# Retention's sample queries: weighting and adding the states on ScalarE and VectorE, then summing by ones, in one core's decoder layer

## The chip, the cores and the metric

The kernel runs on one core of one Trainium2 chip. The metric is the device time of one execution in microseconds (us), the median of several runs. A profiled execution gives the trace from which all other times here are taken; its span runs from its first to its last instruction.

## The reference, cut to what matters

One layer of a hybrid decoder: a feed-forward block, a mixer (retention and HGRN2 side by side), an output projection and a second feed-forward block, for 272 prompt tokens and for 8 sample tokens, each of which has states of its own. The change is in the mixer's work for the 8 samples. For each of them, and for each of the 8 retention heads, a state S of 256 x 256 is updated, and the query reads the new state:

```python
o = jnp.einsum('bhij,bhjv->bhiv', inner, v) + jnp.einsum('bhid,bhdv->bhiv', q_dec, S)
S_new = jnp.exp(lg * C)[:, None, None].astype(S.dtype) * S + jnp.einsum('bhjd,bhjv->bhdv', k_dec, v)
```

With one token per sample (C = 1) the output is q times the new state: a sum over the 256 rows of the state, which lie as two chunks of 128 partitions. The new states are outputs too (`state_ret_sample`). All data is fp32.

## The kernel before, in words

Every large product is a stream of weight blocks. A unit of 8 blocks (128 x 1024, 512 KB) is loaded by SyncE's DMA queue (SP) into `raw`, ScalarE casts its high part into `whi` (L188), VectorE makes the low part `wlo` (L189), and TensorE makes three matmuls per block in L218: `whi` with the high and the low part of the activations, and `wlo` with the high part. `raw`, `whi` and `wlo` have three buffers each. Of a block TensorE reads `whi` first and `wlo` with the third matmul; the next `raw` load of a buffer waits until `wlo` was made from it.

In the mixer, `project` runs over the heads u = 0 to 7: six groups of the input projection (f, q_h, i_h, q_r, k_r, v_r), then four groups of gates of the head before (g_r with a_r, g_h with a_h, twice). A group has 16 steps (k), a step six matmuls, a unit of weights four steps. Beside it run threads, Python generators that `pump` calls once per step: `mix_hg(u)` starts behind i_h, `mix_ret(u)` behind v_r. `yield n` lets n steps pass. So TensorE's order is written out by these numbers; ScalarE's, VectorE's, GpSimd's and SP's orders are made by a scheduler that takes each instruction when it holds it for ready, whatever the step at which it was written.

`mix_ret` keeps the 8 states of a head as four tiles `smr` of 4 samples: `sms[2 * e + c]` has chunk c of samples 4e to 4e + 3. For each half e, ScalarE scales both tiles by the decay (L1192), VectorE adds value times key, sample by sample (L1198), and SP sends both to the output (L1202, `out_srs`). Later come the queries into the bank `pqr`: 16 matmuls (L1211) of 128 x 32 weights from `qdr`, one of whose 32 columns is the query's chunk, with 256 columns of state; four samples go to four 32-row quarters of the bank. `qdr` is zero but for these columns, which `alone` (L734) writes once per head. Behind the queries come the centring, the transposed outputs `por` and the norms; at the end `done_r` releases the gate's evacuation of the group g_r, and `done_h` that of g_h. `mix_hg` has the like for HGRN2: queries `pq` (L1039), then `po`, norms and `done_h`.

Of the kernel before, what the change touches and what calls it, by code (L numbers as in the profile page):

```python
# [13 lines left out]
AF = mybir.ActivationFunctionType  # L14
ALU = mybir.AluOpType
# [3 lines left out]
P = 128  # L19
# [4 lines left out]
NMETA, SEQ, NS = 16, 256, 8  # L24
# [27 lines left out]
ALONE = 4 * 32 + 1  # L52
# [76 lines left out]
def trunk(ctx: ExitStack, tc: tile.TileContext, A, O):  # L129
    nc = tc.nc  # L130
# [12 lines left out]
    def mx_bank(name):  # L143
        return ps_m.tile([P, 512], F32, tag="mx", name=name)
# [94 lines left out]
    def mul(out, a, b):  # L239
        nc.vector.tensor_tensor(out=out, in0=a, in1=b, op=ALU.mult)  # L240
# [306 lines left out]
    with tc.tile_pool(name="yp", bufs=1) as yp:  # L547
# [7 lines left out]
        with tc.tile_pool(name="mp", bufs=1) as mp:  # L555
# [7 lines left out]
            def tmp(name, shape=(P, T), bufs=1, dt=F32, tag=None):  # L563
                if name in rows:
                    rows[name] = rows[name][1:] + rows[name][:1]
                    return rp.tile(list(shape), dt, tag=rows[name][-1], name=name)
                return mp.tile(list(shape), dt, tag=tag or name, name=name, bufs=bufs)
# [19 lines left out]


            qdh = tmp("qdh", (P, 4, ALONE))
            qdr = tmp("qdr", (P, 4, ALONE))  # L590
            nc.gpsimd.memset(qdh, 0.0)
            nc.gpsimd.memset(qdr, 0.0)
            qdh_at = [qdh.rearrange("p a c -> p (a c)")[:, 256 * h :] for h in range(2)]
            qdr_at = [qdr.rearrange("p a c -> p (a c)")[:, 2 * ALONE * c :] for c in range(2)]
            vsm = tmp("vsm", (P, P))
            vt2 = tmp("vt2", (P, 2, P))
            scr2 = tmp("scr2", (P, NMETA))
# [50 lines left out]
            def evacuate(n, c0, c1, o0, o1, b0, b1):  # L648
# [14 lines left out]
                elif n == "i_h":  # L663
                    v = st.pop("i_h", None)
                    if v is None:
                        v = tmp("v", (P, 2, T))
                        nc.scalar.copy(v[:, 0, :], o0)
                        nc.scalar.copy(v[:, 1, :], o1)

                    start(mix_hg(c0 // 2, st["f"], st["k"], st["q"], v), {0: 20, 2: 46}.get(c0, 4))  # L670
                elif n in ("q_r", "k_r"):
                    sc, w, x0 = (1.0, TL, NMETA) if n == "q_r" else (KSC, T, 0)
# [9 lines left out]
                elif n == "v_r":  # L682
                    v = tmp("v", (P, 2, T))
                    nc.scalar.copy(v[:, 0, :], o0)
                    nc.scalar.copy(v[:, 1, :], o1)
                    start(mix_ret(c0 // 2, st["q_r"], st["k_r"], v), 24 if c0 == 2 else 3)
                elif n in ("g_r", "g_h"):
                    sg = tmp("gs", (P, TL), bufs=2)
                    t = tmp("gt", (P, TL), bufs=2)
                    nc.scalar.activation(sg, o0, AF.Sigmoid)  # L690
                    mul(t, sg, o0)
                    sa = tmp("gs", (P, TL), bufs=2)
                    nc.scalar.activation(sa, o1, AF.Sigmoid)
                    mul(t, t, sa)
                    u, e = divmod(c0, 2)
                    while u not in (done_r if n == "g_r" else done_h):
                        pump()
                    if n == "g_r":
                        y = tmp("y", (P, TL))
                        mul(y, t, on_r[u][:, e, :])  # L700
                        st["y"] = y
                    else:
                        y = st["y"]
                        nc.vector.scalar_tensor_tensor(
                            out=t, in0=t, scalar=ngt[:, c0 : c0 + 1], in1=on_h[u][:, e, :], op0=ALU.mult, op1=ALU.mult)

                        ys[c0] = y if c0 < EARLY else yp.tile([P, TL], F32, tag=f"y{c0}", name=f"y{c0}")
                        add(ys[c0], y, t)
                        if c0 < EARLY:
                            split(yh[c0], yl[c0], y)  # L710
# [22 lines left out]
            def alone(qd, q):  # L733
                nc.vector.tensor_copy(  # L734
                    qd[:, :, : 128 : 32].rearrange("p (c e) j -> p c e j", e=2),
                    q[:, :, SEQ:].rearrange("p c (e j) -> p c e j", e=2))
# [9 lines left out]
            def mix_hg(u, f, k, q, v):  # L746

                calm = 2
# [14 lines left out]
                sms, vbs = [], []  # L763
# [230 lines left out]
                def samples(h):  # L994
                    vb, sm = vbs[h], sms[h]
                    for b in range(NS):
                        at = NMETA + b
                        nc.scalar.activation(sm[:, b, :], sm[:, b, :], AF.Copy, scale=meta[:, h, at : at + 1])
                        nc.vector.scalar_tensor_tensor(
                            out=sm[:, b, :], in0=vb[:, b, :], scalar=meta[:, h, at + NS : at + NS + 1], in1=sm[:, b, :],  # L1000
                            op0=ALU.mult, op1=ALU.add)
                    nc.sync.dma_start(O["sgs"][2 * u + h], sm)
# [15 lines left out]
                for h in range(2):  # L1018
# [7 lines left out]
                    for b in range(2):  # L1026
                        nc.vector.scalar_tensor_tensor(
                            out=S[:, b + 1, :], in0=S[:, b, :], scalar=Tt[:, h, b : b + 1],
                            in1=pst[:, (b + 1) * P : (b + 2) * P], op0=ALU.mult, op1=ALU.add)
                    nc.sync.dma_start(O["sgp"][2 * u + h], S[:, 2, :])  # L1030
                if u == 1:
                    yield 2
                    samples(1)
                yield (8, 11, 45)[min(u, 2)]
                pq = mx_bank("pq")
                for h in range(2):
                    for b in range(NS):
                        j = 32 * (b % 4)
                        nc.tensor.matmul(  # L1039
                            pq[j : j + 32, :P], qdh_at[h][:, 32 * b : 32 * b + 32], sms[h][:, b, :],  # L1040
                            start=h == 0 and b < 4, stop=h == 1 and b >= 4, tile_position=(0, j))
# [26 lines left out]
                calm = calm if u else 0  # L1068
# [16 lines left out]
            def mix_ret(u, q, k, v):  # L1085
# [3 lines left out]
                calm = 2  # L1089
                sms = []  # L1090
# [13 lines left out]
                for c in range(2):  # L1104
# [22 lines left out]
                    for x, g, his, i, lo in todo:  # L1127
                        for hi in his:
                            nc.scalar.activation(hi, x, AF.Copy, scale=g)
                        nc.vector.scalar_tensor_tensor(  # L1130
                            out=lo, in0=x, scalar=g, in1=his[i].bitcast(F32), op0=ALU.mult, op1=ALU.subtract)
                    yield 2
                alone(qdr, q)
                vts = [vt[:, 0], vt[:, 1], vs2]
                vrow = rows_out(vt2.rearrange("p c f -> p (c f)")[16:24, :], 256, "vr")

# [25 lines left out]
                for c in range(2):  # L1162
# [9 lines left out]
                    if c == 0:  # L1172
                        gams = [tmp("gam", (P, 1))]
                        nc.gpsimd.tensor_scalar(
                            out=gams[0], in0=so[:, 0:1], scalar1=GAMMA[u], scalar2=GAMMA[u], op0=ALU.min, op1=ALU.max)
# [13 lines left out]
                for e in range(2):  # L1189
# [3 lines left out]
                    for i in (2 * e, 2 * e + 1):  # L1193
                        for c in range(2):
                            for b in (2 * i, 2 * i + 1):
# [3 lines left out]
                                    out=x, in0=vbs[i][:, b - 2 * i, :], scalar=kk, in1=x, op0=ALU.mult, op1=ALU.add)  # L1199
# [1 line left out]
                    for c in range(2):  # L1201
                        nc.sync.dma_start(O["srs"][u, c, :, 4 * e : 4 * e + 4, :], ss[c])  # L1202
                    yield 1 if e else 10 if u == 0 else 6
                yield (11 if u == 0 else 15) + 2 * calm
                pq = mx_bank("pqr")
                scores(pq[:, 256:], 2)
                for e in range(2):
                    for c in range(2):
                        for j in range(4):
                            b = 4 * e + j  # L1210
                            nc.tensor.matmul(  # L1211
                                pq[32 * j : 32 * j + 32, :256], qdr_at[c][:, 32 * b : 32 * b + 32],
                                sms[2 * e + c][:, j, :], start=e + c == 0, stop=e + c == 2, tile_position=(0, 32 * j))
                mul(scr2[:NB2], pq[:NB2, 256 : 256 + NMETA], dt[:NB2, c2:])
                upper_upper_lower(sc2, scr2[:NB2])
                os = tmp("osr", (P, 256))
# [160 lines left out]
```

## Time and profile before

| | |
|---|---|
| median of 3 runs | 2567.05 us (2566.23 to 2567.45) |
| span of the profiled execution | 2563.9 us |
| TensorE busy (modelled ends) | 2553.4 us, 23424 matmul records |
| VectorE busy | 1702.8 us, 66% |
| ScalarE busy | 1392.2 us, 54% |
| retention's queries, `pqr` (L1211) | 256 records, the first at 859.8, the last at 1698.6 us |
| out_srs (L1202) | 32 DMAs of 512 KB, 6.7 us to landing (median) |

The profiled execution's own time is its span; the runs' median stands 3.15 us above it. An fp32 matmul leaves two records. A matmul's record begins when the one before it is still in the array, so the pace is read from the starts: 0.113 us from one 264-column matmul to the next. A row of a timeline gives start, length, engine, line, operation, tiles and count; in brackets, how long the engine was idle before it and what ended that. Heads follow each other in 126 us; head 3's queries are at 1190.65 us.

### The profile page before, as it was taken

How to read it: one execution, taken by the hardware profiler on the slowest of the kernel's cores; microseconds unless marked ns; L12 is line 12 of the kernel's file. 1: busy time of each engine (PE TensorE's matmuls, PEld its weight loads, DVE VectorE, ACT ScalarE, POOL GpSimd, SP SyncE). 2: the span in 40 equal slices, each digit the busy share in tenths (PEclk: the TensorE clock that was granted, in tenths of full speed). 3: DMA queues.
4: the chain of work that ended last, by engine and by line, in shares of the span. 5: the costliest groups of instructions: out<-in, count | busy, mean ns of one | idle time of the engine just before them, and what ended most of it. 6: DMA issues, size and time to landing. Idle time of an engine off the chain costs nothing.

```text
span 2563.9 us, 56275 instructions
## 1 busy us (share of the span) xinstructions
PE 2553.4 (100%) x23424; PEld 2534.4 (99%) x23424; DVE 1702.8 (66%) x2827; ACT 1392.2 (54%) x2186; POOL 57.0 (2%) x152
## 2 busy tenths in 40 slices
PE   9999999999999999999999999999999999999999
PEld 9999999999999999999999999999999999999998
DVE  6444544475569878777777777777885555556555
ACT  5444444444456767767676666675564444444443
POOL 0000000000000000000000000000000000000000
PEclk9999999999999999999999999999999999999999
DMA  7555555555555876767676767675556565565554
GB/s 244 183 187 183 187 182 184 186 182 186 184 201 180 287 265 232 264 214 260 212 264 215 259 223 255 224 239 188 196 190 197 194 197 195 194 196 195 195 195 149
DMA packets 156897, 536.26 MB, mean 209 GB/s; under 512 B 17952, under 2 KB 25952, under 8 KB 156640
## 3 DMA queue, kind: packets, MB, share of 16 engines
q1 hardware_dynamic: 156352, 532.37, 62.0%
q8 instruction: 183, 3.00, 0.5%
q14 instruction: 74, 0.61, 0.1%
q10 hardware_dynamic: 288, 0.29, 0.0%
HBM read 501.99 MB, written 30.61 MB: 208 GB/s over the span
## 4 chain that ended last, share of the span: by engine, by line
PE 96%; DVE 2%; ACT 0%; issue 0%; DMA 0%; SPq 0%; ACTq 0%; DVEq 0%
PE up L218 36%; PE dn L218 19%; PE pj_i_h L218 3%; PE pj_g_r L218 3%; PE pj_q_h L218 3%; PE pj_g_h L218 3%; PE pj_a_r L218 3%; PE pj_a_h L218 3%; PE pj_f L218 3%; PE pj_q_r L218 3%; PE pj_k_r L218 3%; PE wo L218 3%; PE pj_v_r L218 3%; DVE wlo L189 1%; PE pqr L1211 1%; PE psr L1168 0%
## 5 line engine op out<-in xcount | busy, mean ns | idle before, releaser
L189 DVE TENSOR_TENSOR wlo<-raw,whi 128x1024 fp32r<-128x1024 f32 (+1 forms) x869 | 1062.2, 1223 | 740.7 <-ACT whi L188 737.3
L188 ACT CAST whi<-raw 128x1024 fp32r<-128x1024 f32 (+1 forms) x870 | 905.7, 1042 | 909.2 <-PE up L218 411.0
L218 PE MATMUL up<-xh,whi 128*128 128x280 f32 (+1 forms) x2624 | 725.6, 280 | 0.6 <-ACT whi L188 0.6
L218 PE MATMUL up<-xh,wlo 128*128 128x280 f32 (+1 forms) x2624 | 725.8, 280 | 0.4 <-DVE wlo L189 0.3
L218 PE MATMUL up<-xl,whi 128*128 128x280 f32 (+1 forms) x2624 | 725.4, 279 | 0.0
L218 PEld LDWEIGHTS up<-xh,wlo 128*128 128x128 f32 x2624 | 492.6, 189 | 1.0 <-DVE wlo L189 1.0
L218 PEld LDWEIGHTS up<-xh,whi 128*128 128x128 f32 x2624 | 492.6, 189 | 0.8 <-ACT whi L188 0.8
L218 PEld LDWEIGHTS up<-xl,whi 128*128 128x128 f32 x2624 | 492.6, 189 | 0.0
L218 PE MATMUL dn<-hh,whi 128*128 128x280 f32 (+1 forms) x1376 | 384.7, 280 | 0.0
L218 PE MATMUL dn<-hh,wlo 128*128 128x280 f32 (+1 forms) x1376 | 384.3, 279 | 0.0
L218 PE MATMUL dn<-hl,whi 128*128 128x280 f32 (+1 forms) x1376 | 384.3, 279 | 0.0
L218 PEld LDWEIGHTS dn<-hh,whi 128*128 128x128 f32 x1376 | 260.1, 189 | 0.1
L218 PEld LDWEIGHTS dn<-hl,whi 128*128 128x128 f32 x1376 | 260.1, 189 | 0.1
L218 PEld LDWEIGHTS dn<-hh,wlo 128*128 128x128 f32 x1376 | 260.1, 189 | 0.0
L218 PE MATMUL pj_k_r<-xh,whi 128*128 128x280 f32 x256 | 74.2, 290 | 0.0
L218 PE MATMUL pj_g_r<-xh,whi 128*128 128x264 f32 x256 | 74.0, 289 | 0.0
L218 PE MATMUL pj_v_r<-xh,whi 128*128 128x280 f32 x256 | 73.8, 288 | 0.0
L218 PE MATMUL pj_v_r<-xh,wlo 128*128 128x280 f32 x256 | 72.4, 283 | 0.3 <-DVE wlo L189 0.3
L218 PE MATMUL pj_g_h<-xh,whi 128*128 128x264 f32 x256 | 72.7, 284 | 0.0
L218 PE MATMUL pj_k_r<-xh,wlo 128*128 128x280 f32 x256 | 72.4, 283 | 0.0
L218 PE MATMUL pj_v_r<-xl,whi 128*128 128x280 f32 x256 | 72.3, 283 | 0.0
L218 PE MATMUL pj_k_r<-xl,whi 128*128 128x280 f32 x256 | 72.3, 283 | 0.0
(421 smaller groups left out, 5263.4 us busy)
## 6 DMA issues: line engine op xcount, KB each, us to landing
raw<-in_w_up SPq DMA_DIRECT2D x343, 512.0 KB, 4.1
raw<-in_w_in SPq DMA_DIRECT2D x320, 512.0 KB, 4.3
raw<-in_w_dn SPq DMA_DIRECT2D x172, 512.0 KB, 3.5
smr<-in_sr SPq DMA_DIRECT2D x32, 512.0 KB, 5.0
out_srs<-smr SPq DMA_DIRECT2D x32, 512.0 KB, 6.7
raw<-in_w_out SPq DMA_DIRECT2D x32, 512.0 KB, 3.9
vbr<-vrd SPq DMA_DIRECT2D x32, 256.0 KB, 4.1
smh<-in_sg SPq DMA_DIRECT2D x16, 512.0 KB, 5.2
```

Of the source, the lines that this page charges most:

```text
L188: nc.scalar.copy(hi[:, j:jn, :], raw[:, j:jn, :])
L189: nc.vector.tensor_tensor(out=lo[:, j0:j1, :], in0=raw[:, j0:j1, :], in1=hi[:, j0:j1, :].bitcast(F32), op=ALU.subtract)
L218: nc.tensor.matmul(o, w, t, start=start, stop=stop)
L1211: nc.tensor.matmul(pq[32 * j : 32 * j + 32, :256], qdr_at[c][:, 32 * b : 32 * b + 32], sms[2 * e + c][:, j, :], start=e + c == 0, stop=e + ...
```

## The change

For each half e, ScalarE multiplies chunk 0 of each sample's state by the query of that chunk (a scalar per partition), in place, and VectorE multiplies chunk 1 by its query and adds. TensorE then only sums over the partitions: one matmul per sample, with a table `one` whose 32 columns are zero but for the column of half e. The queries stand 32 steps behind the states' update instead of 15 (head 0) or 19; HGRN2's queries stand 13 steps later in heads 2 to 7, so that both still stand at the same step there.

```diff
             qdh = tmp("qdh", (P, 4, ALONE))
-            qdr = tmp("qdr", (P, 4, ALONE))
+            one = tmp("one", (P, 2, 32))
             nc.gpsimd.memset(qdh, 0.0)
-            nc.gpsimd.memset(qdr, 0.0)
+            nc.gpsimd.memset(one, 0.0)
+            for e in range(2):
+                nc.gpsimd.memset(one[:, e, e : e + 1], 1.0)
...
-                yield (8, 11, 45)[min(u, 2)]
+                yield (8, 11, 58)[min(u, 2)]
                 pq = mx_bank("pq")
...
-                alone(qdr, q)
...
-                yield (11 if u == 0 else 15) + 2 * calm
+                yield 18 + 2 * calm
+                for e in range(2):
+                    s0, s1 = sms[2 * e : 2 * e + 2]
+                    for b in range(4):
+                        g = [q[:, c, SEQ + 4 * e + b : SEQ + 4 * e + b + 1] for c in range(2)]
+                        nc.scalar.activation(s0[:, b, :], s0[:, b, :], AF.Copy, scale=g[0])
+                        nc.vector.scalar_tensor_tensor(
+                            out=s0[:, b, :], in0=s1[:, b, :], scalar=g[1], in1=s0[:, b, :], op0=ALU.mult, op1=ALU.add)
+                    yield 5
                 pq = mx_bank("pqr")
                 scores(pq[:, 256:], 2)
                 for e in range(2):
-                    for c in range(2):
-                        for j in range(4):
-                            b = 4 * e + j
-                            nc.tensor.matmul(
-                                pq[32 * j : 32 * j + 32, :256], qdr_at[c][:, 32 * b : 32 * b + 32],
-                                sms[2 * e + c][:, j, :], start=e + c == 0, stop=e + c == 2, tile_position=(0, 32 * j))
+                    for j in range(4):
+                        nc.tensor.matmul(
+                            pq[32 * j : 32 * j + 32, :256], one[:, e, :], sms[2 * e][:, j, :],
+                            start=e == 0, stop=e == 1, tile_position=(0, 32 * j))
```

The order of instructions around head 3's queries, by engine. Lines behind L600 have other numbers in the changed kernel: the weighting is L1209, the sum L1210, the query matmul L1217. First TensorE before, in the group g_r of gates (`pj_g_r` and `pj_a_r` are its banks, `xh` and `xl` the activations by step):

```order
L218 MATMUL pj_a_r_15214<-xh_10_9275,whi_15276 128x264
L218 MATMUL pj_a_r_15214<-xl_10_9276,whi_15276 128x264
L218 MATMUL pj_a_r_15214<-xh_10_9275,wlo_15277 128x264
L1039 MATMUL pq<-smh,qdh 32x128 x16
L1141 MATMUL pqr<-q_r,k_r 16x16 x2
L1211 MATMUL pqr<-smr,qdr 32x256 x16
L218 MATMUL pj_g_r_15213<-xh_11_9279,whi_15276 128x264
```

And TensorE in the changed kernel, in the group g_h behind it:

```order
L218 MATMUL pj_a_h_15375<-xh_7_9265,whi_15415 128x264
L218 MATMUL pj_a_h_15375<-xl_7_9266,whi_15415 128x264
L218 MATMUL pj_a_h_15375<-xh_7_9265,wlo_15416 128x264
L1040 MATMUL pq<-smh,qdh 32x128 x16
L1141 MATMUL pqr<-q_r,k_r 16x16 x2
L1217 MATMUL pqr<-smr,one 32x256 x8
L218 MATMUL pj_g_h_15374<-xh_8_9269,whi_15485 128x264
```

The queries have moved from behind step 10 of g_r to behind step 7 of g_h, and 8 of 16 matmuls are left. Next ScalarE before, from the casts of two units of weights to the queries' evacuation (`osh`; `gs` is a gate's sigmoid):

```order
L188 CAST whi_15216<-raw_15215 128x8x128
L188 CAST whi_15246<-raw_15245 128x8x128
L690 ACTIVATE gs<-pj_g_h_15035 128x264
L188 CAST whi_15276<-raw_15275 128x8x128
L693 ACTIVATE gs<-pj_a_h_15036 128x264
L188 CAST whi_15354<-raw_15353 128x8x128
L188 CAST whi_15395<-raw_15394 128x8x128
L1043 COPY osh<-pq 128x128
```

ScalarE in the changed kernel at the same place (`whi_15268` is the cast that was `whi_15246`):

```order
L188 CAST whi_15238<-raw_15237 128x8x128
L188 CAST whi_15268<-raw_15267 128x8x128
L1209 ACTIVATE smr<-smr,q_r 128x256
L691 ACTIVATE gs<-pj_g_h_15057 128x264
L188 CAST whi_15298<-raw_15297 128x8x128
L694 ACTIVATE gs<-pj_a_h_15058 128x264
L1209 ACTIVATE smr<-smr,q_r 128x256 x3
L188 CAST whi_15328<-raw_15327 128x8x128
L1209 ACTIVATE smr<-smr,q_r 128x256
L188 CAST whi_15377<-raw_15376 128x8x128
L1209 ACTIVATE smr<-smr,q_r 128x256 x3
L188 CAST whi_15415<-raw_15414 128x8x128
```

Each half's first weighting stands alone between two casts. VectorE in the changed kernel at this place (before, the same rows without L1210):

```order
L189 TENSOR_TENSOR wlo_15269<-raw_15267,whi_15268 128x8x128
L1198 SCALAR_TENSOR_TENSOR smr<-vbr,sro,smr 128x256 x3
L240 TENSOR_TENSOR gt<-gs,pj_g_h_15057 128x264
L1210 SCALAR_TENSOR_TENSOR smr<-smr,q_r 128x256
L189 TENSOR_TENSOR wlo_15299<-raw_15297,whi_15298 128x8x128
L240 TENSOR_TENSOR gt<-gt,gs 128x264
L1210 SCALAR_TENSOR_TENSOR smr<-smr,q_r 128x256
L705 SCALAR_TENSOR_TENSOR gt<-gt,ngt,on_h 128x264
L1210 SCALAR_TENSOR_TENSOR smr<-smr,q_r 128x256
L189 TENSOR_TENSOR wlo_15329<-raw_15327,whi_15328 128x8x128
```

The sums stand singly between the low parts. Last SP's queue before:

```order
L185 DMA raw_15275<-in_w_in 128x1024
L1202 DMA out_srs<-smr 128x1024
L185 DMA raw_15353<-in_w_in 128x1024
L1202 DMA out_srs<-smr 128x1024
L185 DMA raw_15394<-in_w_in 128x1024
L185 DMA raw_15463<-in_w_in 128x1024
L1202 DMA out_srs<-smr 128x1024
L185 DMA raw_15493<-in_w_in 128x1024
```

SP's queue in the changed kernel:

```order
L185 DMA raw_15297<-in_w_in 128x1024
L1202 DMA out_srs<-smr 128x1024
L185 DMA raw_15327<-in_w_in 128x1024
L1202 DMA out_srs<-smr 128x1024
L185 DMA raw_15376<-in_w_in 128x1024
L1202 DMA out_srs<-smr 128x1024
L185 DMA raw_15414<-in_w_in 128x1024
L185 DMA raw_15484<-in_w_in 128x1024
```

The third output, of the second half's first chunk, stands one weight load earlier.

More of the change, by code (lines that the diff above doesn't have):

```diff
@@ L589, in trunk @@
             qdh = tmp("qdh", (P, 4, ALONE))
-            qdr = tmp("qdr", (P, 4, ALONE))
+            one = tmp("one", (P, 2, 32))
             nc.gpsimd.memset(qdh, 0.0)
-            nc.gpsimd.memset(qdr, 0.0)
+            nc.gpsimd.memset(one, 0.0)
+            for e in range(2):
+                nc.gpsimd.memset(one[:, e, e : e + 1], 1.0)
             qdh_at = [qdh.rearrange("p a c -> p (a c)")[:, 256 * h :] for h in range(2)]
-            qdr_at = [qdr.rearrange("p a c -> p (a c)")[:, 2 * ALONE * c :] for c in range(2)]
             vsm = tmp("vsm", (P, P))
```

## The prediction

> **What bounds the kernel now.** I read the page first, then TensorE's waits, then the timelines of five engines around one head's sample queries.
>
> ```profile
> span 2563.9 us, 56275 instructions
> PE 2553.4 (100%) x23424; PEld 2534.4 (99%) x23424; DVE 1702.8 (66%) x2827; ACT 1392.2 (54%) x2186; POOL 57.0 (2%) x152
> PE 96%; DVE 2%; ACT 0%; issue 0%; DMA 0%; SPq 0%; ACTq 0%; DVEq 0%
> PE pt L1116 <- POOL tails L1103: 0.9, 1, 0.9
> PE pj_f L218 <- DVE wlo L189: 0.7, 1, 0.7
> PE pj_v_r L218 <- DVE wlo L189: 0.3, 1, 0.3
> PE psc L1141 <- DVE acch L836: 0.2, 1, 0.2
> ```
>
> The chain is TensorE for 96% of the span. The four wait rows are all of TensorE's waits between 740 and 1740 us (engine, what waited, releaser: total, times, longest), where all eight heads lie: 2.1 us. So TensorE work that goes comes off the end in full, and each new wait of TensorE is added in full. What can make it wait is the weight pipeline: raw block by DMA, its high part by ScalarE (whi, L188), its low part by VectorE (wlo, L189), three buffers of each. How near that is to failing is seen in head 3, around its queries:
>
> ```profile
> 1180.41 1.98 ACT L188 CAST whi<-raw 128x1024 fp32r<-128x1024 f32 x2
> 1182.99 0.39 ACT L690 ACTIVATE gs<-pj_g_h 128x264 f32<-128x264 f32 x1 [0.60 <-PE pj_g_h L218]
> 1185.35 1.05 ACT L188 CAST whi<-raw 128x1024 fp32r<-128x1024 f32 x1 [1.97 <-DMA raw<-in_w_in]
> 1184.59 1.22 DVE L189 TENSOR_TENSOR wlo<-raw,whi 128x1024 fp32r<-128x1024 f32 x1
> 1187.26 1.22 DVE L189 TENSOR_TENSOR wlo<-raw,whi 128x1024 fp32r<-128x1024 f32 x1
> 1185.83 0.28 PE L218 MATMUL pj_g_r<-xh,whi 128*128 128x264 f32 x1
> 1188.53 0.28 PE L218 MATMUL pj_g_r<-xh,whi 128*128 128x264 f32 x1
> 1188.75 0.28 PE L218 MATMUL pj_g_r<-xh,wlo 128*128 128x264 f32 x1
> 1190.65 1.08 PE L1039 MATMUL pq<-smh,qdh 128*32 128x128 f32 x32
> 1191.60 0.42 PE L1211 MATMUL pqr<-smr,qdr 128*32 128x256 f32 x3
> 1191.65 1.89 PE L1211 MATMUL pqr<-smr,qdr 128*32 128x256 f32 x29
> 1193.47 0.38 PE L218 MATMUL pj_g_r<-xh,whi 128*128 128x264 f32 x1
> ```
>
> Start, length, engine, operation. A block takes TensorE 1188.53 - 1185.83 = 2.70 us. The low part of the block of 1188.53 is done at 1188.48 and read at 1188.75: 0.27 us of lead. ScalarE is not busy there; it waits for the weights' DMA. Then the queries take TensorE from 1190.65 to 1193.47 without using weights, and the lead grows by 2.8 us. They stand where the pipeline is emptiest.
>
> **Part 1: fewer query matmuls.** They cost 1193.47 - 1191.60 = 1.87 us for 16 of 256 columns (32 records). Eight remain, of the same shape: 0.93 us less per head, 8 x 0.93 = 7.4 us off TensorE. Bounds: zero to 0.93 per head; I take the top, since the 29 records in 1.89 us are evenly paced. The Trainium skill, TensorEngine Tiling (Array Packing), Key Properties, says that changing the tiling mode drains TensorE. By this rule what is paid per change of mode isn't halved. The row of 1191.60 follows HGRN2's queries without a gap, so entering costs nothing there; leaving may be in the 0.38 of the last row, 0.1 more than the 0.28 of its neighbours. By the rule the sum would be (1.87 - 0.1) / 2 = 0.88 per head, 7.1 in all, instead of 7.4.
>
> The memsets of the table of ones come once, 64 elements wide instead of 516: nothing, on GpSimd, idle 98%. The copy into qdr goes:
>
> ```profile
> L734 DVE COPY qdr<-q_r 128x16 f32<-128x16 f32 x8 | 1.4, 176 | 0.0
> L998 ACT ACTIVATE smh<-smh,meta 128x128 f32<-128x128 f32 x128 | 41.1, 391 | 0.4
> L1192 ACT ACTIVATE smr<-smr,gam 128x1024 f32<-128x1024 f32 x16 | 17.6, 1142 | 9.2 <-POOL gam L1174 9.2
> L1198 DVE SCALAR_TENSOR_TENSOR smr<-vbr,sro,smr 128x256 f32<-128x256 f32 x64 | 27.5, 478 | 1.9 <-DMA vbr<-vrd 1.8
> ```
>
> **Part 2: eight weightings and eight sums per head.** The sum (L1210) has the form of L1198: 0.48 us, 0.40 when they follow each other (five took 2.06), so 3.2 to 3.8 us of VectorE per head. A weighting (L1209) of 256 lies between the rows of 128 and 1024 columns: 391 + 128 x (1142 - 391) / 896 = 498 ns, some 0.4 back to back: 3.2 to 4.0 us of ScalarE. Over a head of 126 us (the first out_srs of heads 3 and 4, below, lie 1306.54 - 1180.31 apart) there is room on both (66% and 54% busy). What counts is what these instructions wait for, and who stands behind them.
>
> **Part 3: the new wait.** A weighting overwrites the updated state, which must first have left by the output DMA (L1202). In the order of ScalarE, the first weighting stands between the cast of the block of 1185.83 and that of 1188.53, whatever the later yield says. The queue of the DMAs, and L1202's landings:
>
> ```profile
> 1179.92 0.33 SPq L185 DMA_DIRECT2D raw<-in_w_in  x1
> 1180.31 0.42 SPq L1202 DMA_DIRECT2D out_srs<-smr  x1
> 1182.72 0.33 SPq L185 DMA_DIRECT2D raw<-in_w_in  x1
> 1183.11 0.50 SPq L1202 DMA_DIRECT2D out_srs<-smr  x1
> 1185.84 3.00 SPq L185 DMA_DIRECT2D raw<-in_w_in  x2
> 1188.89 0.43 SPq L1202 DMA_DIRECT2D out_srs<-smr  x1
> 1306.54 0.42 SPq L1202 DMA_DIRECT2D out_srs<-smr  x1
> DMA to landing us min/median/max: 6.4/6.7/7.3
> ```
>
> First wait, by ScalarE's and VectorE's new order. The state's first chunk is issued at 1180.31, as before, and lands at 6.4 (the least, since it is the first of four): 1186.7. Weighting 0.4, gs 0.3 (0.39 less the overlap with its neighbours), cast 1.05, low part 1.25 with the hand-over: 1189.7. VectorE's gt and first sum run beside the cast. TensorE wants it at 1188.75: it waits 0.95 us.
>
> Second wait. In SP's new order the second half's first chunk goes ahead of the second of the two raw loads of 1185.84; it is issued at about 1186.25 instead of 1188.89 and lands at the median 6.7: 1192.95. The weighting of the second half stands ahead of the cast for the block after next: 0.45 + 1.05 + 1.25 = 2.75, done at 1195.7. TensorE, no longer held up by queries, would read it at 1188.75 + 2 x 2.70 = 1194.15, with the first wait 1195.1: it waits 0.6 more. The casts of the raw blocks behind it have their DMAs landed by then. Then the queries come (13 steps of 0.68 us later) and the lead is back.
>
> So a steady head pays 1.55 and saves 0.93. Heads 2 to 7 have this order; I take head 3 for all six. Head 0 has its own:
>
> ```profile
> 854.47 0.80 SPq L1202 DMA_DIRECT2D out_srs<-smr  x1
> 857.19 1.05 ACT L188 CAST whi<-raw 128x1024 fp32r<-128x1024 f32 x1
> 859.89 1.05 ACT L188 CAST whi<-raw 128x1024 fp32r<-128x1024 f32 x1 [0.83 <-DMA raw<-in_w_in]
> 865.45 0.28 PE L218 MATMUL pj_q_r<-xh,wlo 128*128 128x264 f32 x1
> ```
>
> There four weightings stand between the casts of 857.19 and 859.89 and wait for 854.47 + 6.7 = 861.2; four of 0.4, a copy and K's copy (0.9), cast and low part (2.3) end at 866.0. TensorE would read them at 865.45 less the 1.9 us of queries that have moved away: 863.55. It waits 2.5 us. Head 1 I take as a steady one, 1.55, between nothing and head 0's.
>
> **Part 4: HGRN2's queries later.** From 45 to 58 steps in heads 2 to 7: the same 16 matmuls, still right ahead of retention's. Bound: nothing where the lead holds, up to 2.8 us per head where the cover is gone; that loss is already in the first two waits. Nothing waits for the results sooner: mix_ret of head 7 ends 75 steps after its start where 80 are had, mix_hg 131 of 144. What moves with them (centring, norms, output transposes) costs the same; the row below shows the next thin place.
>
> ```profile
> 1219.81 1.22 DVE L189 TENSOR_TENSOR wlo<-raw,whi 128x1024 fp32r<-128x1024 f32 x1
> 1218.33 1.22 DVE L189 TENSOR_TENSOR wlo<-raw,whi 128x1024 fp32r<-128x1024 f32 x1
> 1220.86 0.28 PE L218 MATMUL pj_f<-xh,wlo 128*128 128x280 f32 x1
> ```
>
> The low part ends at 1219.55 and is read at 1220.86: 1.3 us of lead under the norms' work, which now falls some 9 us later. I take no wait there, with up to 1.5 us per head as the bound.
>
> **Sum.** Heads 2 to 7: 6 x (1.55 - 0.93) = 3.7; head 0: 2.5 - 0.93 = 1.6; head 1: 0.6. Together 5.9 us more: the span goes from 2563.9 to 2569.8. The median of the runs before, 2567.05, lies 3.15 above the span; with that, 2573.0.
>
> **Rivals.** (a) *The output lands in time.* If the first chunk lands within 5.4 us instead of 6.4, the second half's within 5.1 and head 0's within 4.2, no wait is left: 2567.05 - 7.4 = 2559.6. For it, other DMAs of 512 KB do:
>
> ```profile
> raw<-in_w_in SPq DMA_DIRECT2D x320, 512.0 KB, 4.3
> raw<-in_w_dn SPq DMA_DIRECT2D x172, 512.0 KB, 3.5
> ```
>
> Against it: L1202's least is 6.4. The Trainium skill, DMA: Bandwidth & Descriptors, Anatomy of one DMA, fits 2.0 us plus bytes over 436 GB/s (for the GpSimd path): 3.2 us as its estimate, which would be this case; the trace's 6.4 disagrees. (b) *Only the first wait.* The second is shortest (0.6) and hangs on an earlier issue. Then seven heads lose 0.95 - 0.93 = 0.02 each and head 0 its 1.6: 2568.8, no change. (c) *The lead isn't won back.* The norms come at the thin place of 1220 with the lead 2 us lower, TensorE waits 1 to 1.5 us there too: 8 to 12 us more, 2581 to 2585. It decides where the lead behind the queries is under 3 us. (d) *TensorE doesn't gain.* If the eight matmuls are paced by weight loads and drains, half the 7.4 is lost: 2576.7.
>
> **How the numbers follow.** 0.2%, 5.1 us, is about what a measurement of this kernel can tell from no change. Forecast 0.42, (a) 0.13, (b) 0.27, (c) 0.12, (d) 0.06. The predicted time is 2573. The range leaves out the far end of (a) and of (c): 2562 to 2584; the forecast's own, with landings of 6.4 to 7.3 in both places, is 2569 to 2579. Faster by over 0.2% (under 2561.9): 0.13. Within: (b), a quarter of the forecast and some of (a)'s near end: 0.33. Slower: 0.54.
>
> **What would show it.** Right: pqr's matmul records halve to 128; ScalarE's waits name smr L1209 with out_srs as releaser, about 4 us in the first half, 64 weightings near 0.4 to 0.5 us; TensorE's waits between 840 and 1710 us rise from 2 to some 13 us, for pj_g_r and pj_g_h on wlo or whi. Wrong: L1209 with hardly a wait, or TensorE's waits still near 2 us with the span 7 us shorter. Waits of pj_f or pj_q_h behind the queries would be (c); over 1 us per head for the eight matmuls, (d).

## The result, and the profile after

The changed kernel takes 2582.23 us (median of 4 runs, 2581.05 to 2583.77), the kernel before 2566.97: the ratio is 1.006, with a 95% interval of 1.0047 to 1.0072. It is slower by 15.3 us, where 6 were forecast. The profiled spans are 2580.3 and 2563.9 us, 16.4 apart.

The page of the changed kernel, the lines that answer to those of before:

```profile
span 2580.3 us, 56142 instructions
PE 2555.9 (99%) x23296; PEld 2534.3 (98%) x23296; DVE 1725.6 (67%) x2883; ACT 1413.3 (55%) x2250; POOL 57.3 (2%) x154
PE 81%; DVE 7%; DMA 4%; issue 4%; ACT 3%; POOL 0%; SPq 0%; DVEq 0%; ACTq 0%; POOLq 0%
```

VectorE and ScalarE are hardly busier (67 and 55% after 66 and 54%). What changed is the chain: TensorE held 96% of it and now 81%, and DVE, DMA and ACT stand in it. TensorE's waits in the mixer (740 to 1760 us; total, times, longest) come to 16.1 us after 2.1; the eight longest:

```profile
PE pj_g_h L218 <- DVE wlo L189: 3.9, 6, 0.8
PE pj_g_r L218 <- DVE wlo L189: 3.8, 5, 0.8
PE pj_g_r L218 <- ACT whi L188: 1.6, 2, 1.2
PE por L742 <- ACT kept L919: 1.2, 1, 1.2
PE pt L879 <- POOL ends L752: 1.1, 5, 0.2
PE pj_f L218 <- DVE wlo L189: 1.0, 2, 0.7
PE pt L1117 <- POOL tails L1104: 0.9, 1, 0.9
PE pj_q_r L218 <- DVE wlo L189: 0.8, 1, 0.8
```

ScalarE's waits say who is late before `whi` and `wlo` are, and the rows of the weighting, the sum and the query matmul by form what they cost:

```profile
ACT smr L1209 <- DMA out_srs<-smr: 44.8, 14, 6.6
L1209 ACT ACTIVATE smr<-smr,q_r 128x256 f32<-128x256 f32 x64 | 28.6, 500 | 50.8 <-DMA out_srs<-smr 44.8 <-DVE K L240 3.8 <-DVE smr L1210 2.2
L1210 DVE SCALAR_TENSOR_TENSOR smr<-smr,q_r 128x256 f32<-128x256 f32 x64 | 28.8, 479 | 6.3 <-ACT smr L1209 6.3
L1217 PE MATMUL pqr<-smr,one 128*32 128x256 f32 x128 | 8.6, 384 | 0.0
```

In 14 waits ScalarE stands 44.8 us in front of a weighting until the output DMA has landed. Not all of this is lost, since ScalarE's casts wait there for the weights' own DMA too. The first row is the changed kernel, the second a kernel with the same instructions in which nothing waits for the output (e3, below):

```profile
ACT whi L188 <- DMA raw<-in_w_in: 34.3, 22, 2.9
ACT whi L188 <- DMA raw<-in_w_in: 69.2, 43, 3.5
```

So some 35 of the 44.8 us stand in the place of waits that ScalarE has without them. Head 3, on SP, ScalarE, VectorE and TensorE (start, length, engine):

```profile
1187.75 0.42 SPq L1202 DMA_DIRECT2D out_srs<-smr  x1
1195.68 0.51 ACT L1209 ACTIVATE smr<-smr,q_r 128x256 f32<-128x256 f32 x1 [6.58 <-DMA out_srs<-smr]
1196.10 0.37 ACT L691 ACTIVATE gs<-pj_g_h 128x264 f32<-128x264 f32 x1
1196.37 1.03 ACT L188 CAST whi<-raw 128x1024 fp32r<-128x1024 f32 x1
1197.43 1.23 DVE L189 TENSOR_TENSOR wlo<-raw,whi 128x1024 fp32r<-128x1024 f32 x1
1195.95 0.28 PE L218 MATMUL pj_a_r<-xh,wlo 128*128 128x264 f32 x1
1197.45 0.38 PE L218 MATMUL pj_g_r<-xh,whi 128*128 128x264 f32 x1 [1.23 <-ACT whi L188]
1198.71 0.59 PE L218 MATMUL pj_g_r<-xh,wlo 128*128 128x264 f32 x1 [0.77 <-DVE wlo L189]
1199.09 0.43 PE L218 MATMUL pj_a_r<-xh,whi 128*128 128x264 f32 x1
1199.31 0.43 PE L218 MATMUL pj_a_r<-xl,whi 128*128 128x264 f32 x1
```

The weighting begins 7.9 us after the DMA's issue (1195.68 - 1187.75). The weights that the next cast reads were issued just ahead of it, at 1187.37, and took 7.0 us, to 1194.4; so the cast could not have begun before that in any case. The output holds it up by another 1.3 us, the weighting and the gate's sigmoid by 0.7. Gate, cast and low part follow in a chain, and TensorE, which had the block before to work on, stops twice. In the last two rows its matmuls start 0.22 us apart, twice the usual 0.113; that is taken up at the end.

To add up TensorE's time, its matmuls are grouped, and the time from each start to the next start is summed over the mixer. The differences to the kernel before, in us, add up to the difference of the profiled spans in each kernel (within 0.1 us); "pt" are the transposes of values and keys, "pqg" a copy that some experiments add:

| kernel | pqr | L218 | pt | por | pqg | rest | sum |
|---|---|---|---|---|---|---|---|
| changed kernel | -6.9 | +18.3 | +2.1 | +1.9 | | +0.9 | +16.4 |
| e1 move only | 0.0 | +3.2 | +2.1 | +0.7 | | +0.8 | +6.9 |
| e2 no weighting | -6.9 | +2.6 | +2.1 | +3.8 | | -0.1 | +1.6 |
| e10 weighting alone, no wait | -6.9 | +3.1 | +2.0 | +3.9 | | 0.0 | +2.1 |
| e3 weighting and sums, no wait | -6.9 | +4.5 | +2.0 | +3.7 | | +0.5 | +3.8 |
| e6 weighting between | -5.4 | +3.7 | +2.1 | +3.6 | +2.2 | +0.5 | +6.7 |
| e9 combined | -5.5 | +2.9 | -0.2 | 0.0 | +2.2 | +1.6 | +1.1 |
| e12 matmuls alone | -6.9 | +1.7 | 0.0 | +0.5 | | +0.6 | -4.1 |

These are single profiled executions (e3's run was 2.3 us under e3's median); the medians below decide between theories, the table says where.

### The profile page after: what moved, and what is told of

The parts are those of the page before. It is cut to its first block, busy times and chain, and to the rows that moved or that the text cites. A ratio compares the mean times of both kernels' runs of the same rounds, so it can differ in the third digit from the quotient of the medians.

```text
span 2580.3 us, 56142 instructions
## 1 busy us (share of the span) xinstructions
PE 2555.9 (99%) x23296; PEld 2534.3 (98%) x23296; DVE 1725.6 (67%) x2883; ACT 1413.3 (55%) x2250; POOL 57.3 (2%) x154
## 4 chain that ended last, share of the span: by engine, by line
PE 81%; DVE 7%; DMA 4%; issue 4%; ACT 3%; POOL 0%; SPq 0%; DVEq 0%; ACTq 0%; POOLq 0%
PE up L218 36%; PE dn L218 19%; PE pj_v_r L218 4%; DVE wlo L189 3%; PE wo L218 3%; PE pj_k_r L218 3%; PE pj_f L218 3%; DMA out_srs<-smr 2%; PE pj_q_r L218 2%; PE pj_g_h L218 2%; PE pj_a_h L218 2%; PE pj_g_r L218 2%; ACT whi L188 2%; PE pj_a_r L218 2%; PE pj_q_h L218 1%
## 5 line engine op out<-in xcount | busy, mean ns | idle before, releaser
L218 PE MATMUL up<-xh,whi 128*128 128x280 f32 (+1 forms) x2624 | 726.1, 280 | 0.0
L218 PE MATMUL up<-xh,wlo 128*128 128x280 f32 (+1 forms) x2624 | 725.7, 280 | 0.3 <-DVE wlo L189 0.3
L218 PE MATMUL up<-xl,whi 128*128 128x280 f32 (+1 forms) x2624 | 725.6, 280 | 0.0
L218 PEld LDWEIGHTS up<-xh,wlo 128*128 128x128 f32 x2624 | 492.6, 189 | 0.7 <-DVE wlo L189 0.7
L218 PEld LDWEIGHTS up<-xh,whi 128*128 128x128 f32 x2624 | 493.0, 189 | 0.0
L218 PEld LDWEIGHTS up<-xl,whi 128*128 128x128 f32 x2624 | 492.9, 189 | 0.0
L218 PE MATMUL dn<-hh,whi 128*128 128x280 f32 (+1 forms) x1376 | 384.7, 280 | 0.0
L218 PE MATMUL dn<-hl,whi 128*128 128x280 f32 (+1 forms) x1376 | 384.3, 279 | 0.0
L218 PE MATMUL dn<-hh,wlo 128*128 128x280 f32 (+1 forms) x1376 | 384.3, 279 | 0.0
L218 PEld LDWEIGHTS dn<-hh,whi 128*128 128x128 f32 x1376 | 260.1, 189 | 0.1
L218 PEld LDWEIGHTS dn<-hl,whi 128*128 128x128 f32 x1376 | 260.1, 189 | 0.1
L218 PEld LDWEIGHTS dn<-hh,wlo 128*128 128x128 f32 x1376 | 260.1, 189 | 0.0
L218 PE MATMUL pj_g_r<-xh,whi 128*128 128x264 f32 x256 | 74.3, 290 | 1.7 <-ACT whi L188 1.6
L218 PE MATMUL pj_g_r<-xh,wlo 128*128 128x264 f32 x256 | 72.0, 281 | 4.0 <-DVE wlo L189 3.8
L218 PE MATMUL pj_g_h<-xh,wlo 128*128 128x264 f32 x256 | 71.3, 278 | 3.9 <-DVE wlo L189 3.9
L218 PE MATMUL pj_k_r<-xh,whi 128*128 128x280 f32 x256 | 74.5, 291 | 0.0
L218 PE MATMUL pj_v_r<-xh,whi 128*128 128x280 f32 x256 | 73.8, 288 | 0.0
L218 PE MATMUL pj_g_h<-xh,whi 128*128 128x264 f32 x256 | 72.6, 284 | 0.5 <-ACT whi L188 0.5
L218 PE MATMUL pj_v_r<-xh,wlo 128*128 128x280 f32 x256 | 72.4, 283 | 0.3 <-DVE wlo L189 0.3
L218 PE MATMUL pj_k_r<-xh,wlo 128*128 128x280 f32 x256 | 72.4, 283 | 0.0
```

Source lines behind the costliest of these rows:

```text
L218: nc.tensor.matmul(o, w, t, start=start, stop=stop)
```

## The experiments

Theory W: the weightings, in ScalarE's order ahead of casts, wait for the output DMA of the state that they overwrite, and TensorE starves. Rival M: the later place of the queries costs the time. Rival L: the added instructions cost it by their length.

**e1: the move alone.** In the kernel before:

```diff
-                yield (8, 11, 45)[min(u, 2)]
+                yield (8, 11, 58)[min(u, 2)]
...
-                yield (11 if u == 0 else 15) + 2 * calm
+                yield 28 + 2 * calm
```

> The kernel before with its 16 query matmuls, but with the queries at the steps of the changed kernel (32 steps behind the update; HGRN2's 13 steps later); no weightings, no sums. Theory W (the weightings make ScalarE wait for the output's DMA, which starves TensorE): the move alone costs only the new small waits of por, pt and ptm, up to 5 us: 2567 to 2573. Rival M (the later place of the queries costs the time, since their cover for the weight pipeline is gone): 15.3 us and the 6.9 us saved by fewer matmuls on top, 2585 to 2590. Rival L (128 more instructions per... half of them on each of ScalarE and VectorE cost it by their length): 2567 to 2573, as W.

Measured: 2572.1 us, ratio 1.0018 (1.0009 to 1.0027), 5.0 us more than before. M falls as the main cause, but the move is not free.

**e2: no weightings, no sums**, from the changed kernel:

```diff
-                for e in range(2):
-                    s0, s1 = sms[2 * e : 2 * e + 2]
...
-                    yield 5
+                yield 5
+                yield 5
```

> The changed kernel without the weightings and the sums: TensorE sums chunk 0 of the states as it is, so the samples' retention output is another. Everything else stays, the later places too. W and L: 2567 less 6.9 for fewer matmuls, plus up to 5 for moved steps: 2560 to 2566. M: the loss stays, 2580 to 2583.

Measured: 2566.7 us, ratio 0.9998 (0.999 to 1.0007). That is 0.7 us above what W and L expected, since the move costs more than was allowed for. Weightings and sums with their waits cost 2582.2 - 2566.7 = 15.5 us.

**e3: the wait taken away.** In the changed kernel the output DMAs of chunk 0 read chunk 1, so that this output is another:

```diff
-                        nc.sync.dma_start(O["srs"][u, c, :, 4 * e : 4 * e + 4, :], ss[c])
+                        nc.sync.dma_start(O["srs"][u, c, :, 4 * e : 4 * e + 4, :], ss[1])
```

> The changed kernel, but the output DMA of chunk 0 sends chunk 1 in its place (that output is another): as many DMAs and bytes, and all weightings and sums, but nothing that is sent is overwritten, so ScalarE has no DMA to wait for. W: TensorE's waits for whi and wlo go, 2560 to 2567. L: the instructions are still there, 2578 to 2582. M: 2580 to 2583.

Measured: 2571.9 us, ratio 1.0016 (1.0007 to 1.0024). With the same instructions and as many DMAs, 10.3 us are gone. ScalarE's only waits in front of a weighting are now short ones for the update itself:

```profile
ACT smr L1209 <- DVE smr L1198: 6.3, 11, 2.8
```

So the wait for out_srs is the largest part, 10.3 of 15.5 us; W's own number was missed, since it left nothing for the move and the sums. The scheduler also put the weightings earlier here, which belongs to taking the wait away: head 3's first begins at 1179.55 us, and the output is issued only at 1184.14. SP's order around the outputs of heads 3 and 4 is the changed kernel's, with the third output ahead of a weight load; so that order does not carry the 10.3 us.

**e10: weightings without sums**, else as e3:

```diff
                         nc.scalar.activation(s0[:, b, :], s0[:, b, :], AF.Copy, scale=g[0])
-                        nc.vector.scalar_tensor_tensor(
-                            out=s0[:, b, :], in0=s1[:, b, :], scalar=g[1], in1=s0[:, b, :], op0=ALU.mult, op1=ALU.add)
```

> As e3 (nothing that is sent is overwritten), but without the sums on VectorE; the samples' retention output is another. e2 without either took 2566.7, e3 with both 2571.9. If the sums carry the 5 us: 2566 to 2568.5. If the weightings on ScalarE do: 2570 to 2573.

Measured: 2567.1 us, ratio 1.0 (0.9991 to 1.0009), 0.4 above e2. ScalarE's 64 weightings cost nothing that can be told when nothing blocks them; the sums on VectorE cost 4.8 us by the medians, 1.7 by the two spans. Their price is between these; a part of L holds.

**e4: the weighting later.** The scheduler had put the weightings ahead of the step at which they are written. Here they read their factors from a copy that TensorE makes at that step:

```diff
+                    pg = mx_bank("pqg")
+                    nc.tensor.matmul(pg[:, :8], ident, q[:, :, SEQ + 4 * e : SEQ + 4 * e + 4], start=True, stop=True)
+                    gq = tmp("gq", (P, 8), bufs=2)
+                    nc.vector.tensor_copy(gq, pg[:, :8])
...
-                        g = [q[:, c, SEQ + 4 * e + b : SEQ + 4 * e + b + 1] for c in range(2)]
+                        g = [gq[:, 4 * c + b : 4 * c + b + 1] for c in range(2)]
```

> The changed kernel, complete, with the weights of each half taken from a copy of the query columns that TensorE makes (one matmul of 8 columns per half) at the step at which the weighting is written: ScalarE's scheduler can't put the weightings earlier than that, some 8 us later than in the changed kernel, when the output has landed. W: ScalarE's wait for out_srs is under 1 us per head instead of 6, TensorE's new waits go, the 16 added matmuls cost 1 to 3 us: 2562 to 2570. L and M: 2580 to 2584.

Measured: 2593.85 us, ratio 1.0107 (1.0094 to 1.0121), slower still, where W expected 2562 to 2570. No weighting waits for out_srs any more, but a new wait stands in TensorE's list:

```profile
PE pqr L1221 <- DVE smr L1214: 14.1, 10, 3.9
```

The first weighting of head 3 came at 1213.20 us, the last after 1217.77, and the query matmuls, from 1218.8 us on, waited for the sums. The wait had only changed its place.

**e6: the weighting between.** As e4, with the copies at steps 14 and 22 behind the update (e4: 22 and 27), the queries at 32 as in the changed kernel:

```diff
-                yield 18 + 2 * calm
+                yield 14
...
-                    yield 5
+                    yield 10 if e else 8
```

> As e4, with the query columns copied 8 steps earlier for the first half and 5 earlier for the second, the query matmuls at the step of the changed kernel. Theory W: in e4 the weightings came so late that the query matmuls waited for the sums (26 us); placed between the landing of the output and the queries they wait for neither, so the time is that of e3 (2571.9, no DMA to wait for) plus 1 to 3 for the added matmuls: 2571 to 2576. Rival: ScalarE has no room at all between the casts there, then TensorE's waits for whi and wlo stay: 2580 and more.

Measured: 2571.9 us, ratio 1.0019 (1.0011 to 1.0028). With nothing left out, it takes what e3 takes: 10.3 us less than the changed kernel. Only a short wait for the sums is left, and ScalarE waits in front of a weighting for its factors alone:

```profile
PE pqr L1221 <- DVE smr L1214: 0.5, 1, 0.5
ACT smr L1213 <- DVE gq L1210: 21.2, 15, 1.7
```

So W is shown from both sides: the wait taken away by other data (e3), and by another place of the same instruction (e6). The copies cost 2.2 us of TensorE (pqg).

**e5: HGRN2's queries alone 13 steps later**, in the kernel before:

```diff
-                yield (8, 11, 45)[min(u, 2)]
+                yield (8, 11, 58)[min(u, 2)]
```

> The kernel before with one thing changed: HGRN2's queries 13 steps later. The move of both queries cost 5.0 us. If HGRN2's part carries it: 2570 to 2573. If retention's part carries it (or the two together, since TensorE loses its cover only when both go): 2566 to 2568.5.

Measured: 2571.0 us, ratio 1.0016 (1.0007 to 1.0025), 4.0 more. It also parts the two queries, which otherwise stand together, so not all of it belongs to the later place. What surely does is pt's 2.0 us, which stands in every kernel with HGRN2 at 58 steps and in none with 45. Of e5, TensorE's wait, and GpSimd's two copies for the transposes:

```profile
PE pt L878 <- POOL ends L751: 1.1, 5, 0.2
1632.20 0.97 POOL L750 COPY ends<-v 128x32 f32<-128x32 f32 x1 [3.50 <-ACT v L668]
1633.12 0.41 POOL L751 COPY ends<-v 128x32 f32<-128x32 f32 x1
1633.02 0.43 DVE L240 TENSOR_TENSOR Q<-Q,T 128x256 f32<-128x256 f32 x1
```

and the same copies before, where VectorE has no instruction from 1627.84 to 1628.63:

```profile
1626.93 0.97 POOL L750 COPY ends<-v 128x32 f32<-128x32 f32 x1 [4.39 <-ACT v L668]
1627.84 0.20 POOL L751 COPY ends<-v 128x32 f32<-128x32 f32 x1
```

VectorE's order is another there: a product now runs beside the second copy, and this takes 0.41 instead of 0.20 us (more on it at the end).

**e11: HGRN2's queries back at 45 steps** in the changed kernel (the first line of e1's diff, reversed).

> The changed kernel with HGRN2's queries back at the step of before. If the move's price adds to the rest: 2582.2 - 4.0 = 2578. If these queries, which need no weights, also fill the place in which TensorE waits: 2573 to 2577. If HGRN2's place does not matter beside the wait: 2581 to 2583.

Measured: 2581.2 us, ratio 1.0057 (1.0043 to 1.0071), 1.0 less than the changed kernel, within the spread of the runs. Beside the wait the place of these queries hardly matters; pt's 2.1 and por's 1.9 us are gone, and L218 and the norms' pvr (2.7) have taken most of them over.

**e8: earlier queries.** As e6, with the copies at 14 and 20 steps, retention's queries at 27, HGRN2's at 45:

```diff
-                    yield 10 if e else 8
+                    yield 7 if e else 6
...
-                yield (8, 11, 58)[min(u, 2)]
+                yield (8, 11, 45)[min(u, 2)]
```

> As e6, with retention's queries 27 steps behind the update instead of 32 and HGRN2's at the step of before (45). If the move's 5 us come from the late places, W: 2566 to 2571. If the queries then wait for the sums again: 2575 and more.

Measured: 2575.1 us, ratio 1.0033 (1.0021 to 1.0046). Between the output's landing and the queries the sums no longer fit in two places:

```profile
PE pqr L1221 <- DVE smr L1214: 5.5, 2, 3.9
```

**e7: out of place.** The weighted chunk goes to two small buffers of its own, and a matmul follows each sum by a step:

```diff
+                        w = tmp("swr", (P, 256), bufs=2)
-                        nc.scalar.activation(s0[:, b, :], s0[:, b, :], AF.Copy, scale=g[0])
+                        nc.scalar.activation(w, s0[:, b, :], AF.Copy, scale=g[0])
                         nc.vector.scalar_tensor_tensor(
-                            out=s0[:, b, :], in0=s1[:, b, :], scalar=g[1], in1=s0[:, b, :], op0=ALU.mult, op1=ALU.add)
+                            out=w, in0=s1[:, b, :], scalar=g[1], in1=w, op0=ALU.mult, op1=ALU.add)
+                        yield 2 if b == 3 else 1
+                        nc.tensor.matmul(
+                            pq[32 * b : 32 * b + 32, :256], one[:, e, :], w,
+                            start=e == 0, stop=e == 1, tile_position=(0, 32 * b))
```

> The changed kernel, complete, with the weighted chunk written into a buffer of its own (two of 128 x 256), so that nothing that is on its way out is overwritten; each sample's matmul follows a step or two behind its sum. W: no wait of ScalarE for out_srs, the time as in e3, 2568 to 2574. Rival (the single matmuls between the projections cost more than the eight in a row, 0.1 us and more for each entry and exit): 2574 to 2582.

Measured: 2625.5 us, ratio 1.0227 (1.0213 to 1.0241), far outside both. One lone query matmul among the projections:

```profile
1220.56 0.28 PE L218 MATMUL pj_a_r<-xl,whi 128*128 128x264 f32 x1
1220.67 0.28 PE L218 MATMUL pj_a_r<-xh,wlo 128*128 128x264 f32 x1
1220.88 0.62 PE L1216 MATMUL pqr<-swr,one 128*32 128x256 f32 x2
1221.43 0.38 PE L218 MATMUL pj_g_r<-xh,whi 128*128 128x264 f32 x1
```

From 1220.67 to 1221.43 are 0.76 us; less 0.113 for the projection's own matmul, the lone one costs 0.65 us. Eight in a row cost 0.12 each (7.83 us for all 64 in the changed kernel). That is 0.53 us for each entry and exit: 56 more of them make 30 of the 56.5 us. Of the rest 15.1 us are waits of the queries for the sums, behind weightings that wait for the two buffers. The experiment says nothing on W.

**e12: fewer matmuls alone.** The kernel before with the eight matmuls by ones and the steps of before, no weightings or sums:

```diff
-                                pq[32 * j : 32 * j + 32, :256], qdr_at[c][:, 32 * b : 32 * b + 32],
-                                sms[2 * e + c][:, j, :], start=e + c == 0, stop=e + c == 2, tile_position=(0, 32 * j))
+                            pq[32 * j : 32 * j + 32, :256], one[:, e, :], sms[2 * e][:, j, :],
+                            start=e == 0, stop=e == 1, tile_position=(0, 32 * j))
```

> The kernel before with eight query matmuls by ones in place of sixteen, at the steps of before, without weightings and sums (chunk 0 alone is summed, so the samples' retention output is another). It is the most that the change could bring. If TensorE's 6.9 us come off in full: 2560 to 2560.5. If they are less as between e1 and e2 (5.4), because other work is waited for behind the shorter queries or the cover of the weights' chain shrinks: 2561 to 2564. If nothing is left: 2566 to 2568.

Measured: 2562.3 us against 2567.4, ratio 0.9981 (0.9972 to 0.999). This is the most that the change could bring, 5.1 us: 6.9 come off the queries, and 2.8 come back in other rows, of which 1.7 in L218, probably since the chain of weights has less cover.

**e9: combined.** As e6, HGRN2's queries at 45 and retention's por 4 steps later in heads 0 and 1:

```diff
-                yield (8, 11, 58)[min(u, 2)]
+                yield (8, 11, 45)[min(u, 2)]
...
-                yield 7
+                yield 7 if u > 1 else 11
```

> As e6, complete, with HGRN2's queries back at the step of before and, in heads 0 and 1, retention's por 4 steps later, where TensorE waited 2.5 us for osr. If the parts add up: 2571.9 - 4.0 - 2.5 = 2565.4, so 2564 to 2568, no slower than before. If they do not (a wait that is taken away turns up elsewhere): 2570 to 2574.

Measured: 2569.4 us, ratio 1.001 (1.0001 to 1.0019), between the two expectations: pt's 2.1 and por's 3.6 us are gone, and some comes back, 0.7 us of it in HGRN2's queries (pq), which no longer stand together with retention's. It is the best version found that leaves nothing out, 12.8 us under the changed kernel and at best level with the kernel before. No version that does the change's work was faster than before.

## Why the prediction was right in direction and small in size

By the medians, in steps from one kernel to the next: fewer matmuls -5.1 (before to e12), the later place +4.4 (e12 to e2), weightings +0.4 (e10), sums +4.8 (e3), wait for the output +10.3 (changed kernel). The first is a gain as forecast, the last is the cause that was forecast; what was taken at nothing between them makes up the difference. The steps add up to 14.8 of the 15.3 us, since the kernel before came out 0.5 us higher beside e12. The first and the last alone give +5.2, near the forecast 5.9.

The time, 2582.2 us, lies inside the stated 2562 to 2584, but outside the forecast's own 2569 to 2579. That it lies inside is luck: the upper end was set for rival (c), whose mechanism is not there.

**Part 1** forecast -7.4 and measured -6.9 in the rows of pqr (14.74 to 7.83 us). The 64 matmuls that went (8 per head) were full price; what isn't halved is 0.46 us, 0.06 per head. The prediction's estimate with the drain at a change of mode, by the Trainium skill, TensorEngine Tiling (Array Packing), Key Properties, was 7.1, and the trace lies nearer to it than to 7.4; that the 0.06 is a drain is not shown. e7 has the price of a lone matmul among projections, 0.53 us per entry and exit, and does not separate a drain from the rest of it. Rival (d) falls: the matmuls kept their 379 ns.

**Part 2** had the weighting at 498 ns (500 measured) and the sum at 0.48 us (0.479). Right as durations, and for ScalarE right as cost. For VectorE "there is room" was the mistake: the sums stand in the same queue as `wlo`, and cost 2 to 5 us.

**Part 3** is the mechanism that was shown. Forecast were 7 x 1.55 + 2.5 = 13.4 us; the runs put the wait at 10.3 by the medians of e3 and e6, and at 12.5 by the spans of the changed kernel and e3. TensorE's gaps in L218 (starts over 0.25 us apart, less 0.113) come to 14.6: 0.9 in head 0, 2.4, 2.5, 2.6, 1.8, 2.0, 1.5 and 0.9 in heads 1 to 7; not all of them are this wait. The 0.9 at 1446.2 us in head 5 stands behind ScalarE's decay, which had waited for the load of the state:

```profile
1443.89 1.15 ACT L1192 ACTIVATE smr<-smr,sro 128x1024 f32<-128x1024 f32 x1 [2.28 <-DMA smr<-in_sr]
1446.00 1.23 DVE L189 TENSOR_TENSOR wlo<-raw,whi 128x1024 fp32r<-128x1024 f32 x1 [1.79 <-ACT whi L188]
```

The sum is near, the parts are not. In head 0 the wait was 0.9 instead of 2.5. A second wait came in heads 1, 2, 4 and 5, and none in 6 and 7; in head 3 the gaps lie in one place. The first DMA of head 3 took 7.9 us instead of the least value 6.4; the reason given for 6.4, that it is the first of four, did not hold; the first wait, forecast at 0.95 us, is 2.3 there, larger by about as much. The 3.2 us that rival (a) had from the Trainium skill, DMA: Bandwidth & Descriptors, Anatomy of one DMA, were not seen: the landings of out_srs are 5.0, 6.0 and 6.9 us (least, median, most, of the six that the profile tells), and 7.9 in head 3. Missing from the step was what a gap does to the clock, some 1.5 us (below).

**Part 4** failed: "nothing" for the later queries. The move costs 5.0 us alone and 4.4 with fewer matmuls. Its places were not the thin one at 1220 that was looked at. With the move alone (e1) they are pt behind GpSimd's slower copy (2.1 us), L218 (3.2) and por (0.7). With fewer matmuls (e2 against e12) they are pt (2.1), por in heads 0 and 1 behind ScalarE's `kept` and the late osr (3.3) and L218 (0.9). That moved work lands beside other work, on engines that take their instructions in order, was not followed.

**The rivals.** (a) is excluded, since ScalarE waits 44.8 us. (b), only the first wait, describes heads 6 and 7 alone. (c) gave 2581 to 2585, where the result lies, but by a mechanism that is not there: it asked for 1 to 1.5 us more of waiting per head behind the queries, and pj_f waits 1.0 us in all instead of 0.7.

## What to carry to other kernels

An instruction that overwrites a buffer on its way out can carry the DMA's whole landing time to its engine, and to everything behind it in that engine's queue; before moving such work to an idle engine, look at what stands behind it, and where a scheduler really puts it. There is a window for it: after the landing, and early enough that the reader does not wait for it; e6 hits it, e4, 8 and 5 steps of 0.68 us later, is already behind it. Work on TensorE that needs no weights is probably also a refill for the weights' chain: taking away 6.9 us of it gave 5.1.

## What the runs showed of the hardware that was not expected

**Two short gaps close together were followed by half of TensorE's clock.** The changed kernel's stretches around the gaps of head 3 (times; PE, PEld, DVE, ACT, POOL busy; granted clock; DMA share; GB/s):

```profile
1196.00:1198.00 2.00, 0.72 (x5) 0.33 (x3) 1.39 (x3) 2.00 (x6) 0.00 (x0) 1.00 0.98 393
1198.00:1199.00 1.00, 0.29 (x1) 0.29 (x2) 1.00 (x3) 1.00 (x4) 0.00 (x0) 0.74 0.64 262
1199.00:1201.00 2.00, 2.00 (x10) 2.00 (x10) 2.00 (x4) 1.16 (x2) 0.00 (x0) 0.50 0.67 207
1202.00:1204.00 2.00, 2.00 (x20) 2.00 (x20) 2.00 (x5) 2.00 (x5) 0.00 (x0) 1.00 0.66 125
```

Two gaps of 1.50 and 1.04 us from start to start, within 2.8 us, were followed by some 3 us at 0.50: 10 matmuls in 2 us instead of 20, an estimated 1.5 us lost on top of the gaps. In head 4, with gaps of 0.33 and 1.04 us, the clock stayed at 1.00. e11 shows it again: in its head 4, gaps of 1.38 and 1.04 us at 1324.30 and 1325.90 were followed by 0.50 (1328 to 1330 us). The Trainium skill, TensorE: Matmul & The Clock Gate, Part 1, names an idle window of about 3.4 us as what takes the clock down; here 2.3 us of idle in two pieces did. It also fits the spread of the runs: e8's took 2571.71, 2575.14 and 2581.11 us at mean clocks of 0.999, 0.998 and 0.997.

**GpSimd's copy of 32 columns** took 0.20 us with VectorE idle and 0.41 with a product of two operands running. In head 1 of the kernel before it took 1.21, beside a whole low part:

```profile
995.45 1.23 DVE L189 TENSOR_TENSOR wlo<-raw,whi 128x1024 fp32r<-128x1024 f32 x1
995.54 1.21 POOL L751 COPY ends<-v 128x32 f32<-128x32 f32 x1
```

In both cases the copy ends within 0.1 us of VectorE's instruction (996.75 and 996.68; in e5 1633.53 and 1633.45), as if it were held until that ends. It is not so beside every VectorE instruction: at 799.47 us it took 0.20 beside a SCALAR_TENSOR_TENSOR (L408), one of whose operands lies in the bank `pj_q_r`. In e9 it began 0.03 us ahead of a product (997.86 and 997.89); there it took 0.20, and the product 0.46 instead of its neighbours' 0.42. That VectorE is the cause was not tested by itself.
